# Two layers of a streaming encoder: three Strassen down stages per feed-forward block in place of two, and an earlier norm

## The chip, the cores and the metric

The kernel runs on one core of a Trainium2 chip. A core has a matrix engine (TensorE, PE in the profile; its weight loads are shown as PEld), a vector engine (VectorE, DVE), a scalar engine (ScalarE, ACT), a general engine (GpSimd, POOL) and a queue engine (SyncE, SP) that starts transfers from memory. The metric is the device time of one execution in microseconds (us); lower is better.

## The reference

The input is 512 tokens of width 1024 in float32. There are two layers, and each does

```python
x = x + 0.5 * swiglu(rms_norm(x, g1), w_gate, w_up, w_down)        # FFN 1
h = rms_norm(x, gm); p = h @ w_in
x = x + concat(attention(p), conv(p)) @ w_out                      # the mix
x = x + 0.5 * swiglu(rms_norm(x, g2), w_gate2, w_up2, w_down2)     # FFN 2
x = rms_norm(x, gp)
# swiglu(x) = (silu(x @ w_gate) * (x @ w_up)) @ w_down, inner width 2816
```

So there are four feed-forward blocks (FFNs), two per layer. All of them have the same sizes: 1024 to 2 x 2816 and back.

## The kernel before

**Layout.** Activations lie transposed, features on the 128 partitions and 512 tokens along the row. The stream `x` is eight blocks of 128 x 512, one for each 128 of the 1024 features. Each float32 factor is split into a rounded high part and a rest (`hi`, `lo`), and each product is three matmuls, hi x hi, hi x lo and lo x hi (`mm3`, lines 193 to 197; the page therefore has three lines 194, 195 and 196 for nearly all matmuls). The split of a weight is a cast on ACT and a subtraction on DVE: `load_w` (lines 155 and 162) for plain weights, `split_into` (lines 284 and 286) for Strassen operands. `split` (lines 201 and 202) does it for activations, `split_scaled` (207 and 208) for the input of the next step.

**An FFN.** The inner 2816 features are 22 blocks, taken as 11 pairs. `CHUNKS` groups the pairs: (0, 2), (2, 5), (5, 8), (8, 11). A chunk first makes the inner activations of its pairs, then adds their down projection to `x`.

- Pairs 0 and 1 are plain: full matmuls of 512 columns (`plain`), then `plain_out` scales by the norm, applies silu and splits (lines 338 to 344). They work on `gx`, the unnormalised input times the gain; the norm's factor comes in afterwards.
- Pairs 2 to 10 go through `pair`, a Strassen-Winograd scheme with seven products of half size (24 matmuls of 256 columns each) in place of eight. It needs sums and differences of the normalised input, which `operands` builds on DVE and ACT (lines 374 to 397) while pair 1 and the first down projection run: `advance(n)` takes n steps of it. The weight sums of a pair are lines 436 to 439 on DVE. `order["pe"]` keeps the products in order on PE.
- The down projections of the first and last chunk are full ones: for each of eight blocks m of `x`, `group` runs three matmuls of 512 columns per inner block, and line 609 adds the result to `x`. For the last chunk, `done(m)` then prepares the next step: the split of the new input and the squares for the next norm, whose sum runs on POOL (line 231). The last two blocks of the very last FFN are done in halves of 256 columns.
- The down projections of the two middle chunks go through `down`, the same scheme with three pairs along the inner side: two groups g of four blocks of `x`, seven products each, 18 matmuls of 256 columns a product; line 500 adds to `x`. For this each pair of the chunk must be turned into sums and differences of quarters (lines 463 to 479).

**The norm.** `Norm()` is called twice. The first call sums the squares with small matmuls (line 238) and takes the root on POOL (line 213). The second spreads the result over the partitions with a matmul (line 257) and copies it to `R` (line 263). `plain_out` and `operands` wait for `R`. In the very first FFN, which starts with the kernel (`w0`), the sums run in pair 0 and the spread in pair 1. After the first layer `NormPost` does the end norm too, and line 1200 multiplies each block of `x` by it in the first chunk.

**Order of the work.** The code is traced in program order; a planner then lays out each engine's own sequence ahead of time from a simulated timeline. It takes work that is ready and prefers what was traced first. `tc.issue_after(i)` places what is traced inside it behind instruction i on its engine. `in_turn` chains all weight casts on ACT, and all weight subtractions on DVE, in traced order. Buffers rotate: three raw weight buffers (`raw`), four quarter buffers (`fr`, which `operands` and `pair` share), four slots each for high and low weight parts, 35 activation slots (`r`), seven PSUM banks (`ps`). SP starts the weight loads in its own order; the accumulating loads of `subtracted` go through POOL's queue (line 418).

Of the kernel before, what the change touches and what calls it, by code (L numbers as in the profile page):

```python
# [7 lines left out]
FP = mybir.dt.float32  # L8
# [7 lines left out]
P = 128  # L16
# [22 lines left out]
RING = 35  # L39
WIDE = 6  # L40
NP = 3
NC = 2
CHUNKS = ((0, 2), (2, 5), (5, 8), (8, 11))
TAPS = (0, 31, 31, 0)
Q = 32
PT = 16
# [35 lines left out]
def encoder_kernel(ctx: ExitStack, tc: tile.TileContext, xT, consts, vecs, rgain, wgu1, wd1, wdq1,  # L82
# [18 lines left out]
    def tmp(w=S, dt=FP):  # L101
        return tmps.tile([P, w], dt, tag="t", name=nm("t"))
# [82 lines left out]
    def low(moved=False):  # L185
        return part(1, moved)

    order = {}

    def ordered(name):  # L190
# [95 lines left out]
        order["lo"] = in_turn(V, lambda: V.tensor_tensor(lo[:, :w], src[:, :w], hi[:, :w].bitcast(FP), ALU.subtract))  # L286
        return hi, lo

    def ffn(l, gx, norm, wgu, wd, wdq, gain, done, w0=None, halved=KD):
        with tc.tile_pool(name="f", bufs=4) as fpool:  # L290
            ffn_body(fpool, l, gx, norm, wgu, wd, wdq, gain, done, w0, halved)

    def ffn_body(fpool, l, gx, norm, wgu, wd, wdq, gain, done, w0, halved):

# [41 lines left out]
        def plain_out(os, R):  # L336
# [84 lines left out]
        def summed(w, src, n=WC, lo=None):  # L421
# [3 lines left out]
            in_turn("h", lambda: A.copy(hi[:, :n], src[:, :n]))  # L425
            return hi, lo

        def pair(p, quartered):

            a11, a12, a21, a22, s3 = quarters(wgu[l, p], WC, p == CHUNKS[0][1])  # L430
            bx, by, bz = bank(), bank(), bank()
            product(bx, split_into("a11", a11), "b11", True, True)
            a = copied(tmp(), bx)
            product(by, summed(wgu[l, p, 1], a12), "b21", True, True)
            with after("first"):
                V.tensor_tensor(s3, a11, a21, ALU.add)
                V.tensor_tensor(a21, a21, a22, ALU.add)  # L437
                V.tensor_tensor(a11, a11, a21, ALU.add)  # L438
# [24 lines left out]
            h0, h1 = slice(0, HS), slice(HS, S)  # L463
            b = slot(FR)
            A.copy(b[:, h0], s[:, h0])
            V.tensor_tensor(b[:, h1], s[:, h0], b[:, h0].bitcast(FP), ALU.subtract)
            b2 = split(s2)
            u, v = fpool.tile([P, S], FP, tag="u", name=nm("u"), bufs=1), tmp()
            V.tensor_tensor(u[:, h0], s[:, h1], s2[:, h1], ALU.subtract)
            order["u0"] = V.tensor_tensor(u[:, h1], u[:, h0], s[:, h0], ALU.subtract).ins  # L470
            V.tensor_tensor(v[:, h0], s[:, h0], s[:, h1], ALU.subtract)
            V.tensor_tensor(v[:, h1], s2[:, h0], u[:, h1], ALU.add)
            us = split(u)
            order["u"] = order["evicted"]
            vs = split(v)
            order["v"], order["vh"] = order["evicted"], order["high"]
            return [{"b11": (b[:, h0], b[:, h1]), "b21": [w[:, h0] for w in b2], "b22": [w[:, h1] for w in b2],
                     "t3": [w[:, h0] for w in us], "t2": [w[:, h1] for w in us],
                     "t1": [w[:, h0] for w in vs], "t4": [w[:, h1] for w in vs]}]

        def down(act, chunk):

# [56 lines left out]
            for _ in range(n):  # L539
                next(steps, None)  # L540

        for p0, p1 in CHUNKS:
            f0, fn = 2 * p0, 2 * (p1 - p0)
            act = []
            last = p1 == NF // 2
            for p in range(p0, p1):
                if p == 0:
                    os = []
                    for r in range(2):
                        ws = w0[2 * r:2 * r + 2] if w0 else [load_w(wgu[l, p, 2 * r + q], WC) for q in range(2)]  # L550
                        os.append([bank(), bank()])
                        if w0 and not r:
                            plain_first(os[r], ws)
                        elif w0:
                            plain(os[r][:1], ws, range(KD))
                            plain([None] + os[r][1:], ws, range(KD // 2))
                            with tc.issue_after(order["mm"]):
                                norm()
                            with after("sums"):
                                plain([None] + os[r][1:], ws, range(KD // 2, KD))  # L560
                        else:
                            plain(os[r], ws, range(KD - 1))
                            plain(os[r], ws, range(KD - 1, KD))
                            if not w0:
                                R = norm()
                    if not w0:
                        scaled(os, R)
                elif p < CHUNKS[0][1]:
                    for r in range(2):
                        ws = [load_w(wgu[l, p, 2 * r + q], WC) for q in range(2)]  # L570
                        o = [bank(), bank()]
                        if w0 and not r:
                            with tc.issue_after(order["mm"]):
                                plain(o[:1], ws, KS[:KD // 4])
                            with tc.issue_after(order["mm"]):
                                R = norm()
                            with after("spread"):
                                plain(o[:1], ws, KS[KD // 4:])
                                plain([None] + o[1:], ws, range(KD))
                            scaled(os, R)  # L580
                        else:
                            plain(o, ws, range(KD))
                        advance(8)
                        act.append(plain_out(o, R))
                else:
                    order.setdefault("pe", order["mm"])
                    act += pair(p, p0 > 0 and not last)
            if p0 and not last:
                down(act, (p0 - CHUNKS[0][1]) // NP)
                continue  # L590
            ahead = {}
            if p0 == 0:

                for m in range(3):
                    ahead[m] = bank(), load_w(wd[l, m, :, f0 * P:(f0 + fn) * P], fn * P)
                    group(*ahead[m], act, range(fn - 1), fn)
            for m in range(halved if last else KD):
                if m in ahead:
# [13 lines left out]
            if last:  # L612

                ms = range(halved, KD)
                ws = [load_w(wd[l, m, :, f0 * P:(f0 + fn) * P], fn * P) for m in ms]
# [542 lines left out]
    for l in range(L):  # L1158
# [9 lines left out]
        if l + 1 < L:  # L1168
# [4 lines left out]
            def done2(m):  # L1173
# [127 lines left out]
```

## Time and profile before

| | us |
|---|---|
| median of three runs | 1751.78 (1751.64 to 1752.09) |
| the profiled execution, its time | 1751.95 |
| its span, first to last instruction | 1750.2 |
| PE busy | 1735.9 (99%) |
| DVE busy | 1411.2 (81%) |
| ACT busy | 1076.6 (62%) |
| POOL busy | 381.3 (22%) |

In this trace the four FFNs begin their Strassen products at about 76, 611, 943 and 1476 us. A row of a timeline gives the start, the duration, the engine, the source line, the operation, what is written and read, the shapes, how many instructions are merged and, in brackets, how long the engine had been idle and what ended that. The duration of one instruction includes its run-out: the next can start before it ends, so the distance from start to start is what an engine spends on one. A row of the table by stretches gives the length of the stretch and the busy time of each engine in it, the number of instructions in brackets.

### The profile page before, as it was taken

Reading aid. Unit: us, or ns where it says so; the run is one execution under the profiler, and the core shown is the slowest. Engines: PE = TensorE matmul, PEld = TensorE weight load, DVE = VectorE, ACT = ScalarE, POOL = GpSimd, SP = SyncE. Lnnn points to the kernel's source line nnn. Section 1 sums busy time; section 2 is a strip of 40 time slices with the busy share of each in tenths; the row PEclk is TensorE's granted clock in tenths of the full one; section 3 lists DMA queues with packets and bytes.
Section 4 is the critical chain, followed back from the end, with each engine's and each line's share of the span. In section 5 each row is a group of like instructions: output and inputs, shape, how many; then the busy total and the mean of one; then the engine's idle time right before and its main releaser. Section 6 shows DMA issues by size and latency. Waiting matters only on the chain. (4 is left out here: it accounts for less than half of the span.)

```text
span 1750.2 us, 30816 instructions
## 1 busy us (share of the span) xinstructions
PE 1735.9 (99%) x12294; PEld 1577.0 (90%) x12294; DVE 1411.2 (81%) x1985; ACT 1076.6 (62%) x1663; POOL 381.3 (22%) x315
## 2 busy tenths in 40 slices
PE   9999999999999999999999999999999999999998
PEld 7899999888578899999889999998986788999997
DVE  7888887688964989897679989866989658888873
ACT  5576756467953476766645757554778435767564
POOL 1001000248813001000310010002576410010001
PEclk9999999999999999999999999999999999999999
DMA  5567574324203457675326575743251125675742
GB/s 184 146 153 188 139 200 102 118 90 117 78 19 103 120 154 179 155 177 139 119 73 166 131 201 133 198 112 114 83 149 34 51 87 147 153 186 141 196 107 82
DMA packets 71951, 228.37 MB, mean 130 GB/s; under 512 B 8448, under 2 KB 9600, under 8 KB 71808
## 3 DMA queue, kind: packets, MB, share of 16 engines
q1 hardware_dynamic: 55536, 171.87, 30.6%
q0 software_dynamic: 16128, 54.53, 18.1%
q8 instruction: 96, 1.57, 0.4%
q14 instruction: 47, 0.39, 0.1%
q10 hardware_dynamic: 144, 0.00, 0.0%
HBM read 222.19 MB, written 2.10 MB: 128 GB/s over the span
## 5 line engine op out<-in xcount | busy, mean ns | idle before, releaser
L195 PE MATMUL ps<-r,weights 128*128 128x256 f32 (+1 forms) x2556 | 802.4, 314 | 0.0
L194 PE MATMUL ps<-r,weights 128*128 128x256 f32 (+1 forms) x2556 | 800.0, 316 | 1.5 <-ACT weights L1117 0.8
L196 PE MATMUL ps<-r,weights 128*128 128x256 f32 (+1 forms) x2364 | 748.0, 318 | 2.4 <-DVE weights L162 1.9
L194 PEld LDWEIGHTS ps<-r,weights 128*128 128x128 f32 x2556 | 480.0, 188 | 39.2 <-ACT t L411 2.3
L195 PEld LDWEIGHTS ps<-r,weights 128*128 128x128 f32 x2556 | 480.1, 188 | 35.0 <-issue 1.9
L196 PEld LDWEIGHTS ps<-r,weights 128*128 128x128 f32 x2364 | 443.8, 188 | 38.2 <-DVE weights L162 3.2
L155 ACT CAST weights<-raw 128x1024 fp32r<-128x1024 f32 (+3 forms) x148 | 131.8, 903 | 212.1 <-PE ps L195 101.6
L194 PE MATMUL ps<-xj,weights 128*128 128x256 f32 x864 | 238.5, 276 | 0.0
L195 PE MATMUL ps<-xj,weights 128*128 128x256 f32 x864 | 238.5, 276 | 0.0
L284 ACT CAST weights<-fr 128x1024 fp32r<-128x1024 f32 (+1 forms) x160 | 157.3, 983 | 97.4 <-DVE fr L438 42.7
L418 POOL DMA_DIRECT2D ls<-in_wgu x72 | 62.6, 869 | 707.6 <-ACT ls L417 635.4
L162 DVE TENSOR_TENSOR weights<-raw,weights 128x1024 fp32r<-128x1024 f32 (+3 forms) x132 | 142.6, 1088 | 88.3 <-ACT weights L155 87.3
L286 DVE TENSOR_TENSOR weights<-fr,weights 128x1024 fp32r<-128x1024 f32 (+1 forms) x160 | 182.2, 1139 | 35.3 <-ACT weights L284 35.2
L195 PEld LDWEIGHTS ps<-xj,weights 128*128 128x128 f32 x864 | 162.2, 188 | 0.0
L194 PEld LDWEIGHTS ps<-xj,weights 128*128 128x128 f32 x864 | 162.2, 188 | 0.0
L196 PE MATMUL ps<-xj,ls 128*128 128x256 f32 x576 | 159.0, 276 | 0.0
L286 DVE TENSOR_TENSOR weights<-raw,weights 128x1024 fp32r<-128x1024 f32 (+1 forms) x100 | 113.4, 1134 | 19.9 <-ACT weights L284 19.6
L980 POOL TENSOR_TENSOR y<-y,pr 128x495 f32<-128x495 f32 (+29 forms) x90 | 118.9, 1323 | 47.2 <-ACT pr L978 41.8
L284 ACT CAST weights<-raw 128x1024 fp32r<-128x1024 f32 (+1 forms) x100 | 97.8, 978 | 32.9 <-DVE raw L516 17.9
L417 ACT ACTIVATE ls<-fr 128x1024 fp32r<-128x1024 f32 (+1 forms) x56 | 56.1, 1002 | 88.8 <-PE ps L196 55.5
L196 PEld LDWEIGHTS ps<-xj,ls 128*128 128x128 f32 x576 | 108.1, 188 | 0.0
L231 POOL TENSOR_TENSOR r<-r,t 128x512 f32<-128x512 f32 x45 | 74.1, 1655 | 132.1 <-ACT t L227 131.7
(257 smaller groups left out, 2913.6 us busy)
## 6 DMA issues: line engine op xcount, KB each, us to landing
fr<-in_wgu SPq DMA_DIRECT2D x112, 512.0 KB, 4.4
ls<-in_wgu POOLq DMA_DIRECT2D x72, 512.0 KB, 6.2
raw<-in_wgu SPq DMA_DIRECT2D x62, 512.0 KB, 5.3
fr<-in_wdq SPq DMA_DIRECT2D x48, 384.0 KB, 4.5
ls<-in_wdq POOLq DMA_DIRECT2D x32, 384.0 KB, 5.6
raw<-in_wd SPq DMA_DIRECT2D x32, 384.0 KB, 3.2
raw<-in_wd SPq DMA_DIRECT2D x32, 256.0 KB, 2.8
raw<-in_wcv SPq DMA_DIRECT2D x16, 512.0 KB, 3.3
```

The costliest lines, as they stand in the source:

```text
L155: order["cast"] = in_turn("h", lambda: A.copy(hi[:, :w], raw[:, :w]))
L162: in_turn(e, lambda: e.tensor_tensor(lo[:, :w], raw[:, :w], hi[:, :w].bitcast(FP), ALU.subtract))
L194: T.matmul(o, lh, rh, start=first, stop=False, skip_group_check=free)
L195: T.matmul(o, lh, rl, start=False, stop=False, skip_group_check=free)
L196: order["mm"] = T.matmul(o, ll, rh, start=False, stop=last, skip_group_check=free).ins
L231: (eng or (V if last else G)).tensor_tensor(self.acc, self.acc, sq, ALU.add)
L284: in_turn("h", lambda: A.copy(hi[:, :w], src[:, :w]))
L286: order["lo"] = in_turn(V, lambda: V.tensor_tensor(lo[:, :w], src[:, :w], hi[:, :w].bitcast(FP), ALU.subtract))
L417: A.activation(lo[:, :n], src[:, :n], AF.Copy, scale=-1.0)
L418: G.dma_start(out=lo[:, :n], in_=w, accum_op=ALU.add)
L980: order["conv"] = G.tensor_tensor(ys[c][:, s:], ys[c][:, s:], pr[:, s:], ALU.add).ins
```

## The change

Pair 1 keeps its plain products, but its activations go to two rows of a buffer (`rows`) and through the quartering, so that pairs 1 to 9 are three chunks of three pairs for `down`. Full down projections remain for pair 0 and for pair 10. Pair 10 is computed before the third `down` (`held`), and its weights come as two loads of four blocks each (`load_cols`, `part_w`). The FFN between the layers (FFN 2 of the first layer) takes `SHORT`: two Strassen stages, and a full projection of pairs 7 to 10. In the three FFNs after the first, the sums of the norm are placed behind pair 0's first half (`r` = 0), and the spread behind the first half of `r` = 1.

```diff
-NC = 2
-CHUNKS = ((0, 2), (2, 5), (5, 8), (8, 11))
+NC = 3
+CHUNKS = ((0, 1), (1, 4), (4, 7), (7, 10), (10, 11))
+SHORT = CHUNKS[:3] + ((7, 11),)
+PLAIN = 2
...
+    def load_cols(wd, l, m, f0, fn):
+
+        raw = wpool.tile([P, WC], FP, tag="raw", name=nm("raw"), bufs=3)
+        nc.sync.dma_start(out=raw.rearrange("p (m f) -> p m f", m=4),
+                          in_=wd[l, m:m + 4, :, f0 * P:(f0 + fn) * P].rearrange("m p f -> p m f"))
+        hi, lo = part(0), low()
+        in_turn("h", lambda: A.copy(hi, raw))
+        in_turn(V, lambda: V.tensor_tensor(lo, raw, hi.bitcast(FP), ALU.subtract))
+        return hi, lo
+
+    def part_w(ws, m, fn):
+        return [w[:, m % 4 * fn * P:(m % 4 + 1) * fn * P] for w in ws[m // 4]]
...
-            u = tmp()
+            u = tmp() if into is None else into
             V.tensor_tensor(u, os[1], R, ALU.mult)
             V.tensor_tensor(u, u, s, ALU.mult)
-            return split(u)
+            return split(u) if into is None else into
...
+        def quartered_out(s, s2):
+            h0, h1 = slice(0, HS), slice(HS, S)
+            b = slot(FR)
+            A.copy(b[:, h0], s[:, h0])
+            V.tensor_tensor(b[:, h1], s[:, h0], b[:, h0].bitcast(FP), ALU.subtract)
+            b2 = split(s2)
...
+            us = split(u)
+            order["u"] = order["evicted"]
+            vs = split(v)
...
+        def plain_pair(p, out):
+            nonlocal R
+            for r in range(2):
+                ws = [load_w(wgu[l, p, 2 * r + q], WC) for q in range(2)]
+                o = [bank(), bank()]
...
+                advance(8)
+                out.append(plain_out(o, R, rows[r]))
+
+        R, os, pending, held = None, [], [], None
+        for p0, p1 in chunks:
             f0, fn = 2 * p0, 2 * (p1 - p0)
-            act = []
             last = p1 == NF // 2
...
+            short = held is not None
+            act, pending = (held if short else pending), []
+            if p0 == 0:
...
+                    elif not r:
+                        plain(os[r], ws, range(KD))
+                        with tc.issue_after(order["mm"]):
+                            norm()
+                    else:
+                        with after("sums"):
                             plain(os[r][:1], ws, range(KD))
...
+                        with tc.issue_after(order["mm"]):
+                            R = norm()
+                        with after("spread"):
+                            plain([None] + os[r][1:], ws, range(KD))
+                if not w0:
+                    scaled(os, R)
+                e = fpool.tile([P, WC], FP, tag="e", name=nm("e"), bufs=1)
+                rows = e[:, 0:S], e[:, S:WC]
+                made = []
+                for p in range(1, PLAIN):
+                    plain_pair(p, made)
+                pending = [quartered_out(*made)]
+            else:
+                for p in range(max(p0, PLAIN), p1) if not short else ():
                     order.setdefault("pe", order["mm"])
-                    act += pair(p, p0 > 0 and not last)
+                    act += pair(p, not last)
             if p0 and not last:
+                if p1 + 1 == NF // 2:
+                    held = pair(p1, False)
                 down(act, (p0 - CHUNKS[0][1]) // NP)
                 continue
             ahead = {}
+            if short:
+                wide_w = [load_cols(wd, l, 4 * q, f0, fn) for q in range(2)]
...
-            ffn(l, gx, norm2, wgu2, wd2, wdq2, vv(l, "g2"), done2)
+            ffn(l, gx, norm2, wgu2, wd2, wdq2, vv(l, "g2"), done2, chunks=SHORT)
```

More of the change, by code (lines that the diff above doesn't have):

```diff
@@ L287, in split_into, with ffn, ffn_body @@
         return hi, lo
-    def ffn(l, gx, norm, wgu, wd, wdq, gain, done, w0=None, halved=KD):
+    def ffn(l, gx, norm, wgu, wd, wdq, gain, done, w0=None, halved=KD, chunks=CHUNKS):
         with tc.tile_pool(name="f", bufs=4) as fpool:
-            ffn_body(fpool, l, gx, norm, wgu, wd, wdq, gain, done, w0, halved)
-    def ffn_body(fpool, l, gx, norm, wgu, wd, wdq, gain, done, w0, halved):
+            ffn_body(fpool, l, gx, norm, wgu, wd, wdq, gain, done, w0, halved, chunks)
+    def ffn_body(fpool, l, gx, norm, wgu, wd, wdq, gain, done, w0, halved, chunks):
         fpool.tile([P, 2, S], FR, tag="xj", name=nm("xj"), bufs=WIDE)
@@ L462, in pair @@
                 return [split(s), split(s2)]
[L463 to L479, printed above, removed]
+            return [quartered_out(s, s2)]
         def down(act, chunk):
@@ L543, in ffn_body @@
+        R, os, pending, held = None, [], [], None
+        for p0, p1 in chunks:
             f0, fn = 2 * p0, 2 * (p1 - p0)
-            act = []
             last = p1 == NF // 2
[L546 to L554, printed above, removed]
-                            plain(os[r][:1], ws, range(KD))
[L556 to L585, printed above, removed]
@@ new lines, in ffn_body @@
+            short = held is not None
+            act, pending = (held if short else pending), []
+            if p0 == 0:
+                for r in range(2):
+                    ws = w0[2 * r:2 * r + 2] if w0 else [load_w(wgu[l, 0, 2 * r + q], WC) for q in range(2)]
+                    os.append([bank(), bank()])
+                    if w0 and not r:
+                        plain_first(os[r], ws)
+                    elif w0:
+                        plain(os[r][:1], ws, range(KD))
+                        plain([None] + os[r][1:], ws, range(KD // 2))
+                        with tc.issue_after(order["mm"]):
+                            norm()
+                        with after("sums"):
+                            plain([None] + os[r][1:], ws, range(KD // 2, KD))
+                    elif not r:
+                        plain(os[r], ws, range(KD))
+                        with tc.issue_after(order["mm"]):
+                            norm()
+                    else:
+                        with after("sums"):
+                            plain(os[r][:1], ws, range(KD))
+                        with tc.issue_after(order["mm"]):
+                            R = norm()
+                        with after("spread"):
+                            plain([None] + os[r][1:], ws, range(KD))
+                if not w0:
+                    scaled(os, R)
+                e = fpool.tile([P, WC], FP, tag="e", name=nm("e"), bufs=1)
[4 more added lines that the diff above has]
+                pending = [quartered_out(*made)]
+            else:
+                for p in range(max(p0, PLAIN), p1) if not short else ():
```

26 lines of the change are left out of this document (21 added, 5 removed).

## The prediction

> **What bounds the kernel now.** I read the busy times first, then the table by stretches, then the timelines of PE (TensorE) and DVE (VectorE).
>
> ```profile
> span 1750.2 us, 30816 instructions
> PE 1735.9 (99%) x12294; PEld 1577.0 (90%) x12294; DVE 1411.2 (81%) x1985; ACT 1076.6 (62%) x1663; POOL 381.3 (22%) x315
> ...
> L194 PEld LDWEIGHTS ps<-r,weights 128*128 128x128 f32 x2556 | 480.0, 188 | 39.2 <-ACT t L411 2.3
> ```
>
> PE is busy for 99% of the span, so time falls only where matmuls go, and only as far as PE is then still fed. DVE at 81% is an average. In the table below the first two rows are two of the four stretches from "norm spread" to "first Strassen product", one in each feed-forward block (FFN); the third is a down stage. The sum rows are over all four starts: everything, then the operand sums of pair 2 alone (L436 and L437 give the same row, L438 the last).
>
> ```profile
> core 0: us, PE busy (x) PEld busy (x) DVE busy (x) ACT busy (x) POOL busy (x), PEclk, DMA share, GB/s
> 33.00:76.00 43.00, 42.10 (x185) 34.02 (x184) 41.46 (x65) 20.96 (x35) 1.94 (x2) 1.00 0.47 127
> 899.00:943.00 44.00, 44.00 (x197) 36.45 (x196) 43.41 (x68) 22.17 (x35) 1.78 (x2) 1.00 0.46 126
> 219.00:247.00 28.00, 28.00 (x248) 27.95 (x248) 26.67 (x38) 15.80 (x21) 2.59 (x3) 1.00 0.76 193
> ...
> sum 173.00, PE 171.09 PEld 140.14 DVE 166.71 ACT 85.42 POOL 7.30; mean PE 42.77 PEld 35.04 DVE 41.68 ACT 21.36 POOL 1.82
> ...
> sum 173.00, DVE 4.87; mean DVE 1.22
> ...
> sum 173.00, DVE 3.55; mean DVE 0.89
> ```
>
> The reader should see two engines full at once: at the four starts PE works 171.09 of 173.00 us and DVE 166.71. Elsewhere DVE has a little room (26.67 of 28.00 in a down stage). PE has its clock throughout (PEclk 1.00).
>
> **The gain: fewer columns.** The rows are the first and last of 21 matmuls of 512 columns, and of 24 of 256.
>
> ```profile
> 50.20 0.39 PE L196 MATMUL ps<-r,weights 128*128 128x512 f32 x1
> ...
> 54.74 0.39 PE L195 MATMUL ps<-r,weights 128*128 128x512 f32 x1
> ...
> 299.95 0.28 PE L194 MATMUL ps<-xj,weights 128*128 128x256 f32 x1
> ...
> 302.56 0.28 PE L196 MATMUL ps<-xj,ls 128*128 128x256 f32 x1
> ```
>
> One of 512 takes 4.54 / 20 = 0.227 us of PE, one of 256 takes 2.61 / 23 = 0.1135. A full down projection of three pairs is 3 x 2 x 8 x 3 = 144 of the first, 32.7 us. A Strassen stage is 2 groups x 7 products x 6 x 3 = 252 of the second, 28.6 us. Three of the four FFNs get one stage more: 3 x 4.1 = **12.2 us less PE work**. The FFN with SHORT swaps full chunks of 2 + 3 pairs for 1 + 4, so 240 matmuls of 512 stay 240. Gate and up products stay: pair 1 was plain and is plain.
>
> The TensorE page of the Trainium skill ("TensorE: Matmul & The Clock Gate", Back-to-back issue gap) speaks against the change: in a stream of weight loads and matmuls it gives about 81 ns at 128 columns and 131 ns at 512, which makes small matmuls dear. An estimate on the straight line between these is 98 ns at 256, so a stage would cost 24.6 instead of 18.9 us, and three stages 17 us more instead of 12.2 less. The two pitches above, 227 and 113.5 ns, do not agree with it.
>
> **The price at the start of an FFN.** The cover goes: between "R is spread" and pair 2, PE loses the down projection of pair 1, 48 x 0.227 = 10.9 us in each of four FFNs, 43.6 in all. DVE loses almost nothing there. Its sizes:
>
> ```profile
> 219.88 0.42 DVE L469 TENSOR_TENSOR u<-t,t 128x256 f32<-128x256 f32 x1
> 220.22 0.42 DVE L471 TENSOR_TENSOR t<-t 128x256 f32<-128x256 f32 x1
> 220.56 0.68 DVE L202 TENSOR_TENSOR r<-t,r 128x512 fp32r<-128x512 f32 x1
> 221.16 0.42 DVE L470 TENSOR_TENSOR u<-u,t 128x256 f32<-128x256 f32 x1
> ```
>
> From start to start 0.34 us for 256 elements and 0.60 for 512. Away: two splits of pair 1 (1.2) and half of eight weight splits (8 x 0.26 = 2.1). New: pair 1's quarters, five halves (1.7) and three splits (1.8). Net +0.2 us, 0.8 in four.
>
> The norm gives something back in three FFNs; in the first one its place stays.
>
> ```profile
> 553.71 0.94 PE L238 MATMUL ps<-ones,r 128*128 128x1 f32 x8
> ...
> 565.55 1.02 PE L257 MATMUL ps<-t,ones 128*128 128x512 f32 x2
> ...
> 554.94 1.97 POOL L213 TENSOR_TENSOR rtok<-vtok,minus_half 128x4 f32<-128x4 f32 x1 [11.17 <-DVE vtok L245]
> ...
> 556.94 0.69 DVE L253 TENSOR_TENSOR t<-cst,rtok 128x512 f32<-128x512 f32 x1 [0.91 <-POOL rtok L213]
> ...
> 565.28 2.54 DVE L162 TENSOR_TENSOR weights<-raw,weights 128x1024 fp32r<-128x1024 f32 x2 [7.65 <-ACT weights L155]
> ```
>
> The sums already run at the end of r=0; new is that the spread runs half of r=1 earlier, 24 x 0.227 = 5.4 us. Its operand is there at 557.6, before the forced place at about 559.9, so PE, whose second half of r=1 is queued behind the spread, should not wait. But the two weight splits at 565.28 wait for PE to free their slots and now fall behind R: 2.5 us of DVE come into the stretch. Head start 2.9 us, three times: 8.7.
>
> What DVE had to spare in the four stretches is its idle time, 173.00 - 166.71 = 6.3, and work for pair 2 done ahead, 4.87 + 4.87 + 3.55 = 13.3: together 19.6. So PE would wait 43.6 - 8.7 - 19.6 + 0.8 = **16 us** if DVE does all older work before the split of pair 2's first operand (a11). Does it?
>
> ```profile
> 72.88 1.22 DVE L286 TENSOR_TENSOR weights<-fr,weights 128x1024 fp32r<-128x1024 f32 x1
> ...
> 75.81 0.28 PE L194 MATMUL ps<-r,weights 128*128 128x256 f32 x1
> ...
> 939.54 1.22 DVE L286 TENSOR_TENSOR weights<-fr,weights 128x1024 fp32r<-128x1024 f32 x1
> 940.68 0.68 DVE L609 SCALAR_TENSOR_TENSOR x<-ps,x 128x512 f32<-128x512 f32 x1
> 941.28 0.68 DVE L1200 TENSOR_TENSOR x<-x,r 128x512 f32<-128x512 f32 x1
> 941.88 1.22 DVE L438 TENSOR_TENSOR fr<-fr,fr 128x1024 f32<-128x1024 f32 x1
> ```
>
> The a11 split ends at 74.1, 1.7 us before PE needs it. At 941.28 L1200 of an older step goes ahead of L438, whose last input was free when L286 ended at 940.8, so the order leans to older work. Upper end: evictions that now come before a11 too, 7 of 32 and 3 of L1200, 10 x 0.6 = 6, so 22. Lower end: the quarters of pair 1 (3.5 x 4 = 14), not needed before the first down stage, slip behind a11: 2. I take 14, near the middle value, since the row at 941.28 speaks for older work first and a few evictions still come late.
>
> **Inside the added stages** I count nothing: a stage as it stands has PE at 28.00 of 28.00, with DVE's work under it in 26.67. If the new stage had some 5% more for DVE, that room of 1.3 us would be gone and each per cent over would cost 0.3 us. The pair held back (10) runs before the last stage and covers pair 9's quarters. A stage brings eight weight loads on SP's queue and four accumulating ones on POOL's:
>
> ```profile
> ls<-in_wdq POOLq DMA_DIRECT2D x32, 384.0 KB, 5.6
> ```
>
> That is 12 x 384 KB where the full projection has 8 x 384, with the DMA engines at a share of 0.76 in a stage that PE does not wait in: nothing on the path.
>
> **The price at the end of an FFN.** The last chunk shrinks from 18 to 6 matmuls per column block, 8 x 6 x 0.227 = 10.9 us for eight.
>
> ```profile
> 317.17 0.68 DVE L609 SCALAR_TENSOR_TENSOR x<-ps,x 128x512 f32<-128x512 f32 x1
> 317.77 0.74 DVE L208 SCALAR_TENSOR_TENSOR r<-x,vec,r 128x512 fp32r<-128x512 f32 x1
> ...
> 320.77 3.48 DVE L208 SCALAR_TENSOR_TENSOR r<-x,vec,r 128x512 fp32r<-128x512 f32 x2
> ...
> 320.26 3.43 POOL L231 TENSOR_TENSOR r<-r,t 128x512 f32<-128x512 f32 x2 [13.10 <-ACT t L227]
> ```
>
> Each block asks DVE for an eviction (0.6) and a split that takes 0.7 alone and 1.74 beside a POOL add: 8 x 1.3 to 8 x 2.3, 10 to 19 us. PE has the mix's first two groups without their last block as cover, 2 x 21 x 0.227 = 9.5. So 0 to 3 us at each of the two passages to the mix; I take 1. At the tail five POOL adds of 1.7 must keep up with 1.36 us per block: 5 x 0.34 = up to 2; I take 1.
>
> ```profile
> 218.81 0.28 PE L194 MATMUL ps<-r,weights 128*128 128x256 f32 x1
> ...
> 240.33 0.96 DVE L286 TENSOR_TENSOR weights<-raw,weights 128x768 fp32r<-128x768 f32 x1
> ...
> 241.31 0.33 SPq L318 DMA_DIRECT2D raw<-in_wgu  x1
> ...
> raw<-in_wd SPq DMA_DIRECT2D x32, 384.0 KB, 3.2
> ```
>
> The two wide loads of the last chunk wait on SP's queue for a raw buffer, with the mix's first loads behind them. The second gets its buffer after the stage's last a12 split, here at 241.3 with PE's stage running to 218.8 + 28.6 = 247.4; 3.2 us of landing, cast and split fit with the first four blocks (5.4 us) ahead of it. Price 0; with that cover gone about 2 us each.
>
> **Sum.** -12.2 + 14 + 2 x 1 + 1 = +4.8. The profiled execution took 1751.95 us (span 1750.2), 0.2 above the median of 1751.78; 1751.95 + 4.8 gives **1757 us**.
>
> **Rivals.** A change of 0.2% (3.5 us) is about what a measurement of this kernel can tell from none.
> *The planner defers.* Pair 1's quarters and the evictions go behind a11. The starts cost 2 to 5 us, the ends 1: -12.2 + 4 + 1 gives **1745**. For it: in the down stage at 219.00 DVE serves both the stage and the next pair, and PE never waits. Against it: the row at 941.28. It decides once all waits are under 12.2 - 3.5 = 8.7 us.
> *A wash.* Starts of about 10 and ends of 2: **1752**.
> *The weight load is not hidden* at 256 columns: 252 x 0.188 = 47.4 against 32.7 us per stage, +44 in three, 1796. The pitch of 0.1135 speaks against it, and so against the skill's rule above, which needs the same thing.
> *The move of the norm does nothing*, because the spread's operand is late: 8.7 us more wait, 1766. The chain above ends 2.3 us early.
>
> **Numbers.** Forecast 0.46 (1753 to 1766 with the ends above), deferral 0.30, wash 0.19, late norm 0.04, weight load 0.01. Range **1743 to 1766**: it takes in deferral and all but the far end of the forecast. Faster 0.30; same 0.19; slower 0.51.
>
> **What would show it.** Matmul count up by 300 (3 x 108, less 24 at the halved tail), PE busy sum down by about 12 us. Right: PE rows at the four starts that wait on DVE L286, 2 to 6 us each, and DVE at 43 of 43 there. Wrong, if a11's split comes before the quarters of pair 1 and PE's waits stay under 8.7; wrong upward, if PE waits at the ends for L208, or at the tail for L231.

## The result, and the profile after

The changed kernel takes 1772.06 us (median of four runs, 1770.24 to 1774.23) against 1751.71 for the kernel before (1750.48 to 1752.09): a ratio of 1.012, 95% interval 1.0108 to 1.0132. It is 20.3 us slower; the forecast was 5 us slower, with a range that ended at 1766. The sign was right and the size was not. The profiled execution below is the slowest of its four, so it lies 22.3 us above that of the kernel before.

The profiled execution of the changed kernel took 1774.23 us. Its page begins with the span and the busy times:

```profile
span 1772.4 us, 31729 instructions
...
PE 1734.6 (98%) x12594; PEld 1588.8 (90%) x12594; DVE 1482.1 (84%) x2117; ACT 1107.5 (62%) x1717; POOL 388.1 (22%) x327
```

There are 300 matmuls more, as foretold. The added stages run as the old ones did. This is the table by stretches over the first down stage of the first FFN and part of what follows it (columns as in the prediction's table):

```profile
218.00:260.00 42.00, 42.00 (x369) 41.87 (x369) 35.80 (x45) 28.89 (x38) 4.32 (x5) 1.00 0.75 191
```

PE is busy for 42.00 of 42.00 us, so nothing is lost there. The loss is at the four starts. The next two tables have the 57 us that follow the spread of the norm in each FFN, first of the kernel before, then of the changed one:

```profile
33.00:90.00 57.00, 56.10 (x309) 48.02 (x307) 50.90 (x75) 30.55 (x47) 2.81 (x3) 1.00 0.52 143
...
sum 228.00, PE 225.96 PEld 195.62 DVE 204.65 ACT 124.48 POOL 10.74; mean PE 56.49 PEld 48.90 DVE 51.16 ACT 31.12 POOL 2.69
```

```profile
33.00:90.00 57.00, 49.11 (x261) 41.73 (x260) 52.72 (x83) 30.31 (x50) 2.80 (x3) 0.94 0.41 112
569.00:626.00 57.00, 51.86 (x272) 44.75 (x271) 51.67 (x81) 31.38 (x50) 2.65 (x3) 0.94 0.44 118
902.00:959.00 57.00, 51.88 (x240) 42.50 (x239) 50.47 (x84) 26.73 (x45) 2.94 (x4) 0.94 0.34 90
1441.00:1498.00 57.00, 50.90 (x247) 42.04 (x246) 50.22 (x80) 28.20 (x45) 1.96 (x3) 0.99 0.35 95
sum 228.00, PE 203.75 PEld 171.02 DVE 205.07 ACT 116.61 POOL 10.35; mean PE 50.94 PEld 42.76 DVE 51.27 ACT 29.15 POOL 2.59
```

PE is idle for 24.3 us of 228 where it was idle for 2.0. DVE works as much as before, 205.07 against 204.65, and is not full either. A finer count adds up how far the distances from start to start of the matmuls go beyond their usual 0.227 and 0.1135 us. From 47 us before pair 2's first product to 20 us behind it, it gives some 5.5 us in the four starts before and 39.6 after: **34 us lost**, about 10, 7, 8 and 9 in order. Some 7.6 of these 34 are what matmuls at half clock took beyond their usual distance (last section); nearly all the rest are waits. In each of the parts between the starts the two traces differ by less than 2 us, and by 1 us in all.

What PE waits for, from the table of waits of the changed kernel (lines are shifted: 301 was 286, 164 was 162, 650 was 609; lines 376 and 377 are the split of an operand in `operands`):

```profile
engine line waited for: us in total, times, longest us
PE ps L211 <- DVE weights L301: 6.7, 8, 2.6
PE ps L211 <- DVE weights L164: 5.2, 3, 2.1
PE ps L209 <- DVE x L650: 5.1, 1, 5.1
PE ps L209 <- ACT weights L299: 3.1, 3, 2.1
PE ps L209 <- ACT r L376: 2.9, 1, 2.9
PE ps L210 <- DVE r L377: 2.4, 2, 1.4
```

No single wait carries it: weight splits, an eviction that holds a PSUM bank, casts and operand splits take turns. Why they are late shows in the timeline of DVE in the first FFN (lines 451, 453 and 217 here are the quartering of pair 1, lines 470 to 473 the weight sums of pair 2, which were 436 to 439):

```profile
66.89 1.23 DVE L301 TENSOR_TENSOR weights<-fr,weights 128x1024 fp32r<-128x1024 f32 x1
...
68.62 0.43 DVE L451 TENSOR_TENSOR u<-u,e 128x256 f32<-128x256 f32 x1
...
70.15 0.43 DVE L453 TENSOR_TENSOR t<-e,u 128x256 f32<-128x256 f32 x1
70.73 1.23 DVE L470 TENSOR_TENSOR raw<-fr,fr 128x1024 f32<-128x1024 f32 x1
71.88 0.69 DVE L217 TENSOR_TENSOR r<-u,r 128x512 fp32r<-128x512 f32 x1
72.48 0.69 DVE L217 TENSOR_TENSOR r<-t,r 128x512 fp32r<-128x512 f32 x1
73.08 0.69 DVE L377 TENSOR_TENSOR r<-fr,r 128x512 fp32r<-128x512 f32 x1
73.68 1.29 DVE L377 TENSOR_TENSOR r<-t,r 128x512 fp32r<-128x512 f32 x2
77.15 1.23 DVE L471 TENSOR_TENSOR fr<-fr,fr 128x1024 f32<-128x1024 f32 x1 [2.18 <-DMA fr<-in_wgu]
```

and in that of SP, which starts pair 2's loads:

```profile
67.01 0.33 SPq L333 DMA_DIRECT2D fr<-in_wgu  x1
67.43 0.39 SPq L333 DMA_DIRECT2D raw<-in_wgu  x1
73.79 0.33 SPq L333 DMA_DIRECT2D fr<-in_wgu  x1
```

The operands of the second half of the features (the rows at 73.08 and 73.68) come behind the quartering of pair 1. They hold a quarter buffer, so the last quarter of pair 2's weights is only asked for at 73.79, and at 77.15 DVE itself has waited 2.18 us for it. Before, three of the four sums had begun by 74.61 and PE began pair 2 at 75.81 without a wait:

```profile
67.80 1.22 DVE L436 TENSOR_TENSOR raw<-fr,fr 128x1024 f32<-128x1024 f32 x1
...
71.74 1.22 DVE L437 TENSOR_TENSOR fr<-fr,fr 128x1024 f32<-128x1024 f32 x1
...
74.61 1.21 DVE L438 TENSOR_TENSOR fr<-fr,fr 128x1024 f32<-128x1024 f32 x1
```

Such a wait of a weight sum for its load stands in all four starts of the changed kernel (one line from the table of DVE's waits in each); in the kernel before there is none:

```profile
DVE fr L471 <- DMA fr<-in_wgu: 2.2, 1, 2.2
...
DVE fr L471 <- DMA fr<-in_wgu: 0.6, 1, 0.6
...
DVE raw L470 <- DMA fr<-in_wgu: 2.0, 1, 2.0
...
DVE fr L471 <- DMA fr<-in_wgu: 1.6, 1, 1.6
```

### The profile page after: what moved, and what is told of

Its sections match the earlier page's. It is cut to its first block, busy times and chain, and to the rows that moved or that the text cites. A ratio compares the mean times of both kernels' runs of the same rounds, so it can differ in the third digit from the quotient of the medians.

```text
span 1772.4 us, 31729 instructions
## 1 busy us (share of the span) xinstructions
PE 1734.6 (98%) x12594; PEld 1588.8 (90%) x12594; DVE 1482.1 (84%) x2117; ACT 1107.5 (62%) x1717; POOL 388.1 (22%) x327
## 3 DMA queue, kind: packets, MB, share of 16 engines
q0 software_dynamic: 17856, 59.25, 19.6%
## 5 line engine op out<-in xcount | busy, mean ns | idle before, releaser
L209 PE MATMUL ps<-r,weights 128*128 128x256 f32 (+1 forms) x2656 | 819.5, 310 | 13.1 <-DVE x L650 5.1
L210 PE MATMUL ps<-r,weights 128*128 128x256 f32 (+1 forms) x2656 | 818.8, 308 | 3.9 <-DVE r L377 2.4
L211 PE MATMUL ps<-r,weights 128*128 128x256 f32 (+1 forms) x2392 | 744.8, 313 | 11.9 <-DVE weights L301 6.7
L209 PEld LDWEIGHTS ps<-r,weights 128*128 128x128 f32 x2656 | 502.1, 189 | 46.2 <-issue 8.2
L210 PEld LDWEIGHTS ps<-r,weights 128*128 128x128 f32 x2656 | 502.2, 189 | 34.6 <-DVE r L377 2.9
L211 PEld LDWEIGHTS ps<-r,weights 128*128 128x128 f32 x2392 | 452.5, 189 | 43.5 <-DVE weights L301 8.5
L299 ACT CAST weights<-fr 128x1024 fp32r<-128x1024 f32 (+1 forms) x178 | 172.3, 968 | 88.7 <-DVE fr L472 37.9
L301 DVE TENSOR_TENSOR weights<-fr,weights 128x1024 fp32r<-128x1024 f32 (+1 forms) x178 | 200.1, 1124 | 32.4 <-ACT weights L299 32.4
L157 ACT CAST weights<-raw 128x1024 fp32r<-128x1024 f32 (+4 forms) x124 | 107.2, 875 | 157.7 <-PE ps L210 85.0
L164 DVE TENSOR_TENSOR weights<-raw,weights 128x1024 fp32r<-128x1024 f32 (+4 forms) x108 | 113.1, 1055 | 42.5 <-ACT weights L157 41.9
L301 DVE TENSOR_TENSOR weights<-raw,weights 128x1024 fp32r<-128x1024 f32 (+1 forms) x112 | 125.3, 1119 | 15.0 <-ACT weights L299 14.6
L299 ACT CAST weights<-raw 128x1024 fp32r<-128x1024 f32 (+1 forms) x112 | 107.7, 962 | 42.2 <-DVE raw L534 24.5
L518 DVE SCALAR_TENSOR_TENSOR x<-ps,x 128x512 f32<-128x512 f32 x154 | 105.9, 688 | 15.4 <-PE ps L211 14.8
L433 POOL DMA_DIRECT2D ls<-in_wdq x44 | 38.0, 863 | 342.8 <-ACT ls L432 333.7
```

Of the source, the lines that this page charges most:

```text
L157: order["cast"] = in_turn("h", lambda: A.copy(hi[:, :w], raw[:, :w]))
L164: in_turn(e, lambda: e.tensor_tensor(lo[:, :w], raw[:, :w], hi[:, :w].bitcast(FP), ALU.subtract))
L209: T.matmul(o, lh, rh, start=first, stop=False, skip_group_check=free)
L210: T.matmul(o, lh, rl, start=False, stop=False, skip_group_check=free)
L211: order["mm"] = T.matmul(o, ll, rh, start=False, stop=last, skip_group_check=free).ins
L299: in_turn("h", lambda: A.copy(hi[:, :w], src[:, :w]))
```

## Experiments

Every kernel was measured beside the kernel before on the same chip; the table has the medians and the ratio to the kernel before with its 95% interval.

| run | us | ratio to before |
|---|---|---|
| the change | 1772.06 | 1.012 (1.0108 to 1.0132) |
| norm_only | 1750.10 | 0.9991 (0.9981 to 1.0) |
| old_norm | 1781.93 | 1.0174 (1.0157 to 1.0191) |
| all_short | 1786.19 | 1.0198 (1.0182 to 1.0213) |
| no_quarters | 1757.76 | 1.0038 (1.0023 to 1.0053) |
| deferred | 1764.70 | 1.0079 (1.0064 to 1.0094) |
| no_sums | 1763.97 | 1.007 (1.0055 to 1.0085) |
| warm | 1778.51 | 1.0159 (1.0142 to 1.0175) |
| no_cover | 1735.82 | 0.991 (0.9895 to 0.9925) |
| ends | 1758.67 | 1.0042 (1.0027 to 1.0057) |
| ends_norm | 1759.17 | 1.0046 (1.0031 to 1.0061) |
| ends_late | 1747.56 | 0.9976 (0.9967 to 0.9985) |

**Is the gain of the stages there?** all_short is the changed kernel with this edit:

```diff
-    def ffn(l, gx, norm, wgu, wd, wdq, gain, done, w0=None, halved=KD, chunks=CHUNKS):
+    def ffn(l, gx, norm, wgu, wd, wdq, gain, done, w0=None, halved=KD, chunks=SHORT):
```

> The changed kernel with SHORT in all four FFNs: the starts are those of the change, but no FFN has the third stage, the held pair or the two wide loads. If an added stage saves what its column count says and costs nothing beside it, the time rises by 3 x 4.1 = 12.2 us over the changed kernel, to 1784 (1782 to 1786). If the loss is in the added stages or at the ends of the FFNs, the time stays at 1772 or falls towards 1764.

Measured: 14.1 us more than the changed kernel, 0.2 us above the first forecast's range. Three added stages save what their columns say, 12.2, within the scatter of the runs (some 2 us), and neither the stages nor the shorter last chunk take much of it back.

**The norm, in the old kernel and in the new.** norm_only is the kernel before with the new place of the two norm calls, old_norm the changed kernel with the old one:

```diff
                     elif not r:
                         plain(os[r], ws, range(KD))
-                        with tc.issue_after(order["mm"]):
-                            norm()
                     else:
-                        with after("sums"):
-                            plain(os[r][:1], ws, range(KD))
-                        with tc.issue_after(order["mm"]):
-                            R = norm()
-                        with after("spread"):
-                            plain([None] + os[r][1:], ws, range(KD))
+                        plain(os[r], ws, range(KD))
+                        R = norm()
```

(the two branches shortened; this is old_norm, and norm_only is the reverse.)

> The kernel before, with only the earlier place of the norm's sums and spread in the three later FFNs; two Strassen stages and full down projections of pairs 0 and 1 as before. My theory (the loss sits at the starts, where the cover of pair 1's down projection is gone) gives no change, 1751 to 1753 us: the starts wait for nothing here, and a head start of DVE buys nothing where PE is already full. The rival that the earlier norm itself costs something (the spread holds PE in the middle of pair 0, or the eviction of pair 0 gets in the way) gives 3 us or more over the kernel before.

> The changed kernel with the norm's two calls where they were before, after pair 0's products. In the prediction's sum the earlier norm gave DVE a head start of 2.9 us in each of three FFNs. If that holds, this kernel is 8.7 us slower than the changed one, 1780 to 1782. If the head start is lost in waits, it stays at 1771 to 1774.

Measured: in the kernel before the move is worth between 0 and 3 us (1 us under the forecast of no change); in the changed one taking it back costs 9.9 us. The head start was worth what was counted for it, 8.7, but only where PE waits. The two DVE rows below, of old_norm and of the changed kernel in the second FFN, show it: the first multiplication by the norm is preceded by two weight splits in the one, and stands alone, after a wait for R, in the other.

```profile
568.72 2.54 DVE L164 TENSOR_TENSOR weights<-raw,weights 128x1024 fp32r<-128x1024 f32 x2 [7.64 <-ACT weights L157]
571.17 0.69 DVE L353 TENSOR_TENSOR t<-ps,r 128x512 f32<-128x512 f32 x1
```

```profile
567.61 0.69 DVE L353 TENSOR_TENSOR t<-ps,r 128x512 f32<-128x512 f32 x1 [3.62 <-ACT r L278]
```

**The quartering, left out and put later.** no_quarters feeds the first stage pair 2 twice; deferred does all the work, with the quartering behind pair 2's last weight sum:

```diff
-                pending = [quartered_out(*made)]
+                pending = []
...
+                if len(act) < NP:
+                    act = act[:1] + act
```

```diff
-                pending = [quartered_out(*made)]
...
-                V.tensor_tensor(a12, a12, a11, ALU.add)
+                done_sums = V.tensor_tensor(a12, a12, a11, ALU.add).ins
+            if p == PLAIN:
+                with tc.issue_after(done_sums):
+                    pending.append(quartered_out(*made))
...
```

> The changed kernel without the quartering of pair 1; the first down stage takes pair 2's quarters twice, so pair 1 is missing from the sum and the output is not the reference's. The cover of PE's work is gone as in the change, but DVE and ACT have 3.5 us less to do at each start and i=1's operands are not behind it. Theory A (the quartering, placed ahead of pair 2's operands, is what starves PE): the excess of 35 us at the starts falls by 20 or more, to 1745 to 1753. Theory B (the loss of cover alone starves PE): it falls by no more than 14 us, the quartering's own DVE time, 1758 to 1770.

> The changed kernel with pair 1's quartering placed behind the last weight sum of pair 2 on DVE; all the work of the change is done. Theory A: the four starts get back 3.5 us of DVE each and the operands of i=1 come 3 to 5 us earlier, 14 to 22 us less, 1750 to 1758. Theory B: at most 1766 to 1772. A third way is that the wait only moves behind the first products of pair 2, where the second operand splits then queue behind the quartering: 1766 to 1772 as well, but with the waits between the third and the seventh product of pair 2.

Measured: 14.3 us less without the quartering, which is theory B's limit, and 7.4 us less with it deferred, between the two theories' numbers. 14.3 is close to the quartering's own time on DVE, 4 x 3.5 = 14. That each of these us lies on the path is not shown by it, since the run also takes away the quartering's work on ACT and its place in front of the operands. Theory A's "20 or more" was too much: 20 of the 34 us stay when the quartering is gone. In deferred no weight sum waits for its load any more, in any of the four starts; these waits were 6.4 us together. But there half of the quartering still comes before splits that pair 2 waits for (the row of L301 is one of those):

```profile
72.20 1.22 DVE L473 TENSOR_TENSOR fr<-fr,fr 128x1024 f32<-128x1024 f32 x1
73.33 0.42 DVE L447 TENSOR_TENSOR r<-e,r 128x256 fp32r<-128x256 f32 x1
...
74.94 1.22 DVE L301 TENSOR_TENSOR weights<-fr,weights 128x1024 fp32r<-128x1024 f32 x1
```

**The cover alone.** no_cover is the kernel before with one line more:

```diff
             ahead = {}
             if p0 == 0:
+                act, fn = act[:2], 2
```

> The kernel before without pair 1's part of the first down projection in all four FFNs (48 matmuls of 512 columns less in each, the inner blocks 2 and 3 missing from the sum, so the output is not the reference's); no third stage, no quartering, the norm in its old place. PE has 4 x 10.9 = 43.6 us less work, and DVE loses some 8 us of weight splits, 2.1 in each start. If the kernel before had the 19.6 us of DVE spare that the prediction counted, the starts wait 43.6 - 19.6 - 8 = 16 us or less and the time falls by about 27, to 1724. If there is no spare (theory C: the work done ahead is needed by the pair that follows), the wait is 36 to 44 us and the time stays, 1744 to 1752.

Measured: 15.4 us less than the kernel before on the same chip (1751.24). PE has 43.6 us less to do, so 28 us are lost, between the two forecasts (16 at most, 36 or more). The distances give 31 us at the four starts and 3 less elsewhere. DVE has hardly a pause there (sum row of four stretches, from the spread to between 2 and 12 us behind pair 2's first product):

```profile
sum 156.00, PE 138.28 PEld 113.44 DVE 154.06 ACT 79.56 POOL 6.14; mean PE 34.57 PEld 28.36 DVE 38.52 ACT 19.89 POOL 1.54
```

DVE 154.06 of 156.00; up to the first product alone it is 133.9 of 134.6. So the idle time of DVE was used up. Of the 19.6 us that the prediction counted as spare, 43.6 - 8.4 (weight splits gone from DVE) - 28.2 = 7 could be used (5 by the distances at the starts), about the 6.3 us of idle time and hardly anything of the work done ahead.

**Does every us of DVE count?** After no_quarters it looked so (theory C). no_sums is the changed kernel without the four weight sums of pair 2:

```diff
+                if p > PLAIN:
                     V.tensor_tensor(s3, a11, a21, ALU.add)
                     ...
+                else:
+                    s3 = a22
```

> The changed kernel without the four weight sums of pair 2 in each FFN (its products take wrong factors, so the output is not the reference's): 4 x 1.15 = 4.6 us less DVE work at each start, 18.4 in four, while PE's work and cover are those of the change. Theory C, formed after the first runs (from R on DVE is full, and each us of DVE work that PE has no cover for is a us of wait, also work that was formerly done ahead): 16 to 18 us less, 1754 to 1756. Theory D (the waits are for loads, casts and slots that come late, not for DVE's amount of work): 9 us less or smaller, 1763 or more.

Measured: 8.1 us less, of 18.4 us of DVE work taken away. Theory C in its strict form falls, and theory D, which set 9 us as its bound, fits. With the sums gone DVE itself waits (its waits in the first FFN, 67 to 87 us):

```profile
DVE weights L301 <- ACT weights L299: 4.4, 4, 1.4
DVE t L477 <- PE ps L211: 1.6, 1, 1.6
```

So behind the first products the wait looks like a chain (load, sum, cast, split, product) in which DVE's amount of work is one part. The same shows in the 20 us from the first product on, summed over the four FFNs, of the kernel before and of the changed one:

```profile
sum 80.00, PE 79.88 PEld 79.75 DVE 61.17 ACT 52.94 POOL 6.89; mean PE 19.97 PEld 19.94 DVE 15.29 ACT 13.24 POOL 1.72
```

```profile
sum 80.00, PE 64.66 PEld 61.71 DVE 67.23 ACT 47.19 POOL 7.24; mean PE 16.17 PEld 15.43 DVE 16.81 ACT 11.80 POOL 1.81
```

Before, DVE had 19 us of room there; two or three of the four sums were done or begun by then. After, it does 6 us more, has 12.8 us of room left, and PE still waits 15.

**The clock.** In the changed kernel the granted clock falls to half for some us in each start (last section). warm gives PE spare work in front of pair 2's first product:

```diff
-                    order.setdefault("pe", order["mm"])
+                    if p == PLAIN:
+                        warm = conv_bank()
+                        v = X["b11"][0][0]
+                        with tc.issue_after(order["mm"]):
+                            for _ in range(24):
+                                order["pe"] = T.matmul(warm, v[:, 0:P], v, start=True, stop=True).ins
```

> The changed kernel with 24 spare matmuls of 512 columns (5.4 us, read by nobody) on PE between the first down projection and pair 2's first product, in each FFN; the order on DVE stays that of the changed kernel. They give PE work in part of the stall (about 8.6 us a start) and take no work from DVE. If the half clock after a stall adds to the time, up to the 8 us that matmuls at half clock took beyond their usual distance in the four starts come back: 1764 to 1770 us, and fewer stretches at half clock. If DVE's lag alone sets the time and PE at half clock only fills a wait that is there anyway, the time stays, 1770 to 1774. If the starts are bound by something that begins only when the products begin, the spare matmuls add their 4 x 5.4 = 21.8 us: 1794.

Measured: 6.5 us more (the profiled executions differ by 2.6). Of 21.8 us of spare work some 15 disappeared in waits. By the distances the second and fourth start took all of it in, and the first and third some 2 us less than their 5.4. In the third the longest wait (3.5 us for an eviction) stood ahead of the spare matmuls; in the first the waits came back behind them. None of the three forecasts was met. The matmuls at half clock in the four starts took 4.5 us beyond their usual distance in place of 7.6, and no time came back, so this run gives no sign that half clock made the loss. It holds at most 7.6 of the 34 us, and that it adds a part of these is not excluded.

**The third stage at the other end.** ends keeps both full pairs at the start and puts pairs 8 to 10 through `down` in the first three FFNs; ends_norm adds the earlier norm:

```diff
-NC = 2
+NC = 3
...
-                    act += pair(p, p0 > 0 and not last)
-            if p0 and not last:
+                    act += pair(p, p0 > 0 and not (last and tail))
+            if p0 and not (last and tail):
...
                 add(0, 1, px, 1)
+                for m in range(4 * g, 4 * g + 4) if last else ():
+                    done(m)
```

> The kernel before, with the third Strassen stage at the other end of the FFN: pairs 0 and 1 keep their full down projections, pairs 2 to 10 go through three stages in the first three FFNs (the last one keeps its full end). The starts keep their cover, the saving is the same three stages. If the cover at the starts was the whole loss, and an end costs no more than 1 to 2 us, 1751.6 - 12.2 + 3 to 6 gives 1740 to 1746 us. The rival: the last four blocks of x come only with the last products, DVE then has four evictions, splits and squares to do at once, and an end costs 4 us or more: 1752 or more.

> The same as the run called ends, with the earlier norm of the change in the three later FFNs. The move alone gave 0.9991 (0.9981 to 1.0): 0 to 3 us less than ends. If the end is bound by DVE, the earlier sums wait for the squares of the late blocks, the spread is forced into the middle of pair 0, and the time is above that of ends by up to 3 us.

Measured: 7.3 us slower than before, and the earlier norm changes nothing. That is the rival's number. The four starts lose 5.3 us together by the finer count (5.5 before), so the cover does what was thought. The loss is at the ends, and more than half of it, 11 of some 20 us, at the end of the FFN between the layers, where the sums of the next norm wait for the squares too (4.9 us in two waits). The largest single wait is this (PE in ends, first FFN; three splits for the next step, L208, had gone ahead of L286 on DVE):

```profile
323.18 0.28 PE L195 MATMUL ps<-r,weights 128*128 128x256 f32 x1
327.81 0.58 PE L196 MATMUL ps<-r,weights 128*128 128x256 f32 x1 [4.35 <-DVE weights L286]
```

ends_late has the added stage in the first FFN of each layer only, and puts the next step's preparation behind the stage's last weight split and cast:

```diff
...
+                if last:
+                    with behind([order["lo"], turns["h"]]):
+                        for m in range(KD):
+                            done(m)
```

> The kernel before with a third Strassen stage for pairs 8 to 10 at the end of the two first FFNs of a layer alone (there the mix follows), and with the preparation of the next step placed behind the stage's last weight split on DVE and its last cast on ACT. In the run called ends a single wait of 4.2 to 4.5 us for a weight split stood in each of these two stages, where splits for the next step had gone ahead on DVE. If that order was the cause, the two waits go and 1751.6 - 2 x 4.1 to 4.7 + 1 to 3 gives 1743 to 1747 us. If the end is bound by the amount of DVE work, the wait moves into the mix and the time is 1749 or more.

Measured: 1747.56, 3.7 us less than the kernel before on the same chip, ratio 0.9976 (0.9967 to 0.9985). It is faster than both kernels, and just above the forecast of 1743 to 1747. The wait for L286 is gone, so the order on DVE was its cause. The gain over ends has a second source, which no run separates: ends_late has no added stage in the FFN between the layers, where ends lost most. Two stages should save 8.2 (2 x 4.1). What is left of waits at the two ends is in the table of waits of ends_late, and 8.2 - 4.7 = 3.5 is about what was measured:

```profile
PE ps L195 <- DVE r L208: 4.7, 4, 1.2
```

## Why the prediction was right and wrong

- **What bounds the kernel.** Right: PE alone, with DVE full between the norm and pair 2. By the distances the loss came at the starts and nowhere else.
- **The gain, -12.2.** Right (all_short: 14.1, within the scatter). The rule of the Trainium skill ("TensorE: Matmul & The Clock Gate", Back-to-back issue gap) would have made the stages dearer than the full projection, by the prediction's estimate from it; all_short shows that they are cheaper.
- **Inside the stages 0, ends 3.** The stages cost 0. The ends cost 1.5: two waits for the split of the next step's input (L223, which was L208), one at each passage to the mix, 0.5 and 1.0, where 2 x 1 were counted. The tail costs 0 in place of 1: from the last matmul to the end of the span it is 5.7 us (6.4 before).
- **The norm's head start, 8.7.** Right (9.9). It is not free gain: norm_only shows that it is worth at most 3 us where nothing waits.
- **The quartering, 14.** Right as a size (14.3), though that number holds its place as well as its work. That older work goes first is right in the main: in the second and third FFN the whole quartering stands ahead of a11's split on DVE, in the fourth all but one split, but in the first FFN half of it comes behind (68.62 against 66.89 in the timeline above). The rival that the planner defers is wrong twice: it did so for that part alone, and where the whole quartering is made to wait (the evictions stay where they were), the time is 1764.7 and not 1745.
- **The start of an FFN, 14: here the prediction failed.** The mis-sized term is "what DVE had to spare", 19.6 = 6.3 idle + 13.3 done ahead. By no_cover it is 7, hardly more than the idle part. The 13.3 us done ahead were not a reserve. The timelines suggest why: the sums stand at the head of a chain that ends in pair 2's next products, and done just in time each passes its load, cast and split on to PE as a wait. No run shows this chain by itself; no_sums shows that the amount of DVE work alone doesn't explain it. The room that DVE has during pair 2 (19 us in 80) didn't help: PE waited with 12.8 us of it left.
- **The upper end, 22, was too low.** It allowed for ten evictions in front of pair 2 and no more. What it left out is the place of the quartering ahead of the second half of the operands, which keeps a quarter buffer taken and one of pair 2's loads waiting: deferred gives 7.4 back, and the 6.4 us of waits for loads go with it. A kernel with more quarter buffers was not tried.
- **The sum with the measured terms.** 43.6 + 0.8 - 9.9 - 7 + 7.4 = 34.9 us lost at the starts, where the trace has 34. Less the stages' 12.2 that is +22.7, where the profiled executions differ by 22.3 and the medians by 20.3. The close fit is partly luck: no_sums shows that the terms don't simply add, the sum has no term of its own for the half clock (7.6 us), and each term has some 2 us of scatter. How much of the chain is the late load and how much the cast and split was not separated.
- **What was to show it.** The waits on L286 (301 now) were to be 2 to 6 us each, 16 in all. They are 6.7 in all, and the rest is spread over five other pairs of lines. "DVE at 43 of 43" holds in the first FFN only: from the spread to pair 2 DVE is busy 33.0 of 33 us there, and 38.9 of 40, 41.5 of 45 and 35.2 of 37 in the others. The PE busy sum fell by 1.3 and not by 12, because matmuls after a wait and at half clock are longer in the records; the busy sum was a poor test.

## What to carry to other kernels

Work that the second engine has done ahead is not spare time: before counting it, follow the chain from it to the product that needs it, and ask whether that chain fits when it starts only when it must. When a saving takes away the main engine's work, take it where the other engines have room, here at the end of the first FFN of each layer and not at the starts, and place the next step's preparation behind what the stage itself still needs. A head start for an engine is worth its full length where the main engine waits for it, and little elsewhere.

## What the runs showed of the hardware

In the kernel before, the granted TensorE clock is 1.00 from 6 us to the last matmuls. In the changed kernel it falls to half after waits of a few us. This is the timeline of PE in the first FFN, and the table by stretches over the same place (PEclk is the third number from the end of a row):

```profile
71.81 0.58 PE L209 MATMUL ps<-r,weights 128*128 128x256 f32 x1 [2.90 <-ACT r L376]
73.82 0.58 PE L210 MATMUL ps<-r,weights 128*128 128x256 f32 x1 [1.43 <-DVE r L377]
74.20 0.41 PE L211 MATMUL ps<-r,weights 128*128 128x256 f32 x1
74.41 0.41 PE L209 MATMUL ps<-r,weights 128*128 128x256 f32 x1
```

```profile
62.00:70.00 8.00, 4.71 (x22) 3.36 (x20) 8.00 (x15) 3.38 (x5) 0.98 (x1) 1.00 0.62 146
70.00:77.00 7.00, 3.76 (x16) 3.47 (x17) 4.82 (x8) 2.18 (x4) 0.00 (x0) 0.51 0.37 133
77.00:84.00 7.00, 5.63 (x46) 5.23 (x46) 6.79 (x7) 5.82 (x7) 0.87 (x1) 1.00 0.54 113
```

From 70 to 77 us the granted clock is 0.51, and matmuls of 256 columns start 0.21 us apart in place of 0.1135. PE had not been idle for the whole time before: four products ran between 68.2 and 68.9, and from 66.7 to 70.1 PE was busy for 1.3 of 3.4 us. The stretches at half clock in the four starts last 6.8, 6.8, 6.8 and 3.4 us. The Trainium skill ("TensorE: Matmul & The Clock Gate", What's actually happening) gives the clock a free-running window of 3413 ns and half speed after an idle one. The lengths, one or two times 3.4 us, agree with the window. That the window before has to be idle does not agree if idle means without any matmul: here a mostly idle one was enough.
